# The Mixer's last projection as seven block products, with weight sums made by adding transfers and row loads issued by SyncE

## The chip, the cores and the metric

The kernel runs on one core of one Trainium2 chip. The metric is the device time of one execution in microseconds, as the median of several runs. Engines are named as in the profile: PE is the matrix engine, DVE the vector engine, ACT the scalar engine, POOL GpSimd, SP SyncE, which here issues transfers only.

## The reference, cut to what matters

A trunk layer over 1024 tokens of 1024 channels, in fp32: a mixing sub-layer with two convolution branches, then a gated FFN, each behind a norm and inside a residual. The part around the change:

```python
y_a = jnp.einsum('bsc,cd->bsd', y_a, w_short_out[l])
...
y_b = jnp.einsum('bsc,cd->bsd', u, w_conf_out[l])
g_a, g_b = jnp.split(jax.nn.sigmoid(gate_br), 2, axis=-1)
mix = jnp.einsum('bsd,de->bse', g_a * y_a + g_b * y_b, w_o[l])
x = x + g1 * mix
h2 = rms_norm(x, norm_ffn_g[l]) * (1.0 + sc2) + sh2
a, bgate = jnp.split(jnp.einsum('bsd,df->bsf', h2, w_ffn_in[l]), 2, axis=-1)
x = x + g2 * jnp.einsum('bsf,fd->bsd', jax.nn.silu(a) * bgate, w_ffn_out[l])
```

The vectors `g1`, `sc2`, `sh2` and so on come from `silu(c) @ w_ada + b_ada`, the modulation.

## The kernel before, in words

Activations lie in SBUF with channels on the 128 partitions and tokens along them: 8 rows of channels (`j`) by two halves of 512 tokens (`h`). A matmul multiplies a 128x128 weight block with a 128x512 operand into one PSUM bank.

**fp32 out of three passes.** Each operand is split in a high part and a rest (`split`, L543; `t_split`, L552: a cast on ACT and a subtraction on DVE). So is each weight tile of 128x1024, 512 KB (`split_w`, L234: `wh` by ACT at L244, `wl` by DVE or POOL at L245). `mm3` (L495) then makes three matmuls: wh with xh, wh with xl, wl with xh.

**Seven block products.** Nearly all projections take their matrix in duals: a dual is four weight blocks 11, 12, 21, 22, and its four result blocks are made by seven products instead of eight, the Strassen-Winograd scheme (`PRODUCTS`, the names "1", "2", "6", "5", "7", "3", "4"; `product`, L512). Products 6, 5, 7 and 3 take sums of weight blocks, and 6, 5, 7, 3 and 4 take sums or differences of operand blocks. A product is 24 matmuls. Weights are planned in the list `plan`, and `next_w` (L466) keeps three units begun: the one that is handed out and `AHEAD` = 2 more (`fetch`). In the duals of the second output product (`conf_units`) and of the first, a sum of two weight blocks is a load by SP and an adding transfer onto it, issued by POOL. In the first duals of the FFN (`dual_units`, L251, `begin` at L272 for the second) the sums are made by DVE.

**The stages around the change**, each bound to its order on PE:
- ya, `w_short_out`: two duals, then the gated result stands in the tiles `ma[j, h]`. In it also runs the layer norm of the other branch, on DVE and ACT.
- yb, `w_conf_out`: two duals in `CONF_ORDER`. `yb_evac` (L1391) multiplies the result with the gate rows `gb` (loaded by POOL, `gates_b`) and adds it onto `ma`: by DVE for row 1, half 0 of each block (L1402), by an adding transfer `ma<-gb` of POOL for the others (L1403), twelve in all.
- mix, `w_o`: the one projection that is done directly. `mix(i, h)` (L1463) runs over two halves and eight column blocks: one weight tile and 24 matmuls (`col_block`) each, 384 in all. In the first half the last three weight tiles are kept (`KEPT`) for the second, so that there are 13 loads. Each block loads its rows of x by POOL (`xr`, L1466), evacuates with `x1 = gate*out + xr` on DVE (L1471), stores x1 to DRAM by POOL (L1474), squares it on ACT (L1475) and adds the square to the half's sum on DVE (L1481). Also here run ten of the modulation's blocks, each a load by SP and a multiply with accumulation on DVE (`load_b`, L486).
- The norm before the FFN: `norm_2_first` (L1499) for half 0 after the first block of half 1. Its sum over channels (`parts_sum`) is two matmuls, `ss` at L689, between a split of the sum (`sumh`, `suml`, L682 and L683) and the inverse root on DVE. `norm_2_half` and `norm_2_sums` do half 1 and the operand sums of the FFN's first two duals, on DVE.
- the FFN's first projection, `w_ffn_in`, in eleven duals in `in_order`; its head is the time of the first two.

The order of each engine's instructions is the order of the program, with some moved behind a named instruction (`tc.issue_after`).

Of the kernel before, what the change touches and what calls it, by code (L numbers as in the profile page):

```python
# [40 lines left out]
P = 128  # L41
# [50 lines left out]
S2_AT = (2, 3, 4)  # L92
# [28 lines left out]
CONF_ORDER = [(d, m) for m in "1256" for d in range(2)] + [(0, "3")] + [(d, m) for m in "74" for d in range(2)] + [(1, "3")]  # L121


MOD_FROM = 16

# [14 lines left out]
def block_kernel(ctx: ExitStack, tc: tile.TileContext, x0, xT, c, vecs, ada, w_first, w_plain, w_duals,  # L140
# [110 lines left out]
    def dual_units(mats, n, early=0, eng=nc.vector):  # L251
# [20 lines left out]
        def begin():  # L272

            with tc.issue_after(load.ins):
                get("21", "22")
            yield
            with tc.issue_after(parts.lo):
                eng.tensor_tensor(a["22"], a["21"], a["22"], ALU.add)
            with tc.issue_after(load.ins):
                get("11")  # L280
            yield
            a["s2"] = s2p.tile([P, T], F32, tag="x1", name="s2")[:, :n]
            with tc.issue_after(mix.half_0):
                eng.tensor_tensor(a["s2"], a["11"], a["22"], ALU.add)
            yield
# [70 lines left out]
    def added_units(mats):  # L356


        a = {}
        mat = dict(zip(("11", "12", "21", "22"), mats))  # L360

        def add(raw, b):
            nc.gpsimd.dma_start(raw, mat[b], accum_op=ALU.add)
            return raw

        def unit(m):
            if m == "6":
# [11 lines left out]
            return split_w(raw, 1024)  # L379

        return {m: (lambda m=m: unit(m)) for m in PRODUCTS}
# [3 lines left out]
    def conf_units(mats, d):  # L385
# [15 lines left out]
        def unit(m):  # L401
            if m == "5":
                raw = a["s1"] = add(get("22"), "21")
            elif m == "6":
                lo = split_w.lo
                raw = a["s2"] = get("11", (rawp, rawbp)[d])
                with tc.issue_after(lo):
                    nc.vector.tensor_tensor(raw, raw, a["s1"], ALU.add)
            elif m == "7":
                raw = add(get("21"), "11")  # L410
            elif m == "3":
                raw = add(a["s2"], "12")
            else:
                raw = get({"1": "11", "2": "12", "4": "22"}[m])
            return split_w(raw, 1024, () if m in "12" else (split.act, split.ins))

# [46 lines left out]
    plan += [(w_o[k], 1024) for ks in (range(KC), SECOND[KEPT:]) for k in ks]  # L463
    ready = []

    def next_w(ahead=AHEAD):  # L466

        fetch(ahead + 1)
        return ready.pop(0)
# [73 lines left out]
    def split(src, tile_of, name):  # L543
        hi, lo = tile_of(name + "h", dt=F32R), tile_of(name + "l", dt=F32R)
        split.act = nc.scalar.copy(hi, src).ins
        split.ins = nc.vector.tensor_tensor(lo, src, f32(hi), ALU.subtract).ins
# [5 lines left out]
    def t_split(src, hi, lo):  # L552
# [3 lines left out]
    def minus(out, a, b):  # L556

        nc.vector.scalar_tensor_tensor(out=out, in0=a, scalar=-1.0, in1=b, op0=ALU.mult, op1=ALU.subtract)
# [54 lines left out]

    kept = []

    def first_w(k):

        w = next_w(min(AHEAD, KC - 1 - k))
        if k >= KC - KEPT:
            kept.append(w)  # L620
        return w

    def second_w(i):

        if i < KEPT:
            fetch(i)
            return kept.pop(0)
        return next_w()
# [615 lines left out]
    n_mod = 0  # L1244
    for d, m in win_order:
# [22 lines left out]
        for n in range('55'.count(m) * (BEGUN < d < GATED)):  # L1268
            with tc.issue_after(short_conv.ins):
                modulation_of(MOD_FROM + n_mod, load(ada[MOD_FROM + n_mod], home=(dual_units.home,dual_units.home)[n_mod % 2]))  # L1270
            n_mod += 1
    while late:
        late.pop(0)()

# [11 lines left out]
    def z_split(m, k, src):  # L1286
        tz[m][k] = split(src, hl_tile, "z" + m)
# [24 lines left out]
    def load_b(i):  # L1312

        loaded.append((i, load(ada[i])))
        if len(loaded) > 1:
            with tc.issue_after(split.ins):
                modulation_of(*loaded.pop(0))


# [4 lines left out]
    loaded = []  # L1324
# [45 lines left out]
    for i, (d, m) in enumerate(ya_order):  # L1370
        gates_a(d, m)
        product(ya_banks[d], m, tq[m], ya_evacs[d], onto="2")
        if q_steps:
            q_steps.pop(0)()
        if i == 0:
# [10 lines left out]
    mg = [[None, None] for _ in range(KC)]  # L1386

    def mg_split(o, h):
        mg[o][h] = split(ma[o, h], hl_tile, f"mg{o}{h}")

    def yb_evac(d, banks):  # L1391
# [3 lines left out]
        def out(i, row, h, op, src):  # L1395
            j = 4 * d + 2 * i + row
            g = gbs.pop((j, h))
            op(g, src, g)
            if (row, h) == (1, 0):
                nc.vector.tensor_tensor(ma[j, h], ma[j, h], g, ALU.add)  # L1400
                mg_split(j, h)
            else:  # L1402
# [39 lines left out]
    def z_3(k):  # L1442
# [6 lines left out]
        (0, "4"): lambda: [mg_split(j, 0) for j in range(0, KC, 2)],  # L1449
# [9 lines left out]

# [3 lines left out]
    def mix(i, h):  # L1463
        j = SECOND[i] if h else i
        xr = g_tile("xr")
        nc.gpsimd.dma_start(xr, xT[j, :, halves[h]])  # L1466
        (o,) = col_block((second_w if h else first_w)(i), mg, (h,), "mix", SECOND if h else [*range(0, KC, 2), *range(1, KC, 2)])
        if h == 0:
            x1[j] = ucp.tile([P, T + CK - 1], F32, tag="uc", name=f"x1{j}")[:, :T]
        dst = x1[j][:, halves[h]]  # L1470
        evac = nc.vector.scalar_tensor_tensor(out=dst, in0=o, scalar=modc(16 + j), in1=xr, op0=ALU.mult, op1=ALU.add)  # L1471
        if (i, h) == (KC - 1, 0):
            mix.half_0 = evac.ins
        nc.gpsimd.dma_start(x1_dram[j][:, halves[h]], dst)  # L1474
        sq = nc.scalar.activation(xr, dst, AF.Square, scale=1.0 / 32.0)  # L1475
        if (i, h) == (KC - 1, 1):
            load_rsqrt(sq.ins)
        if i == 0:
            sums[h] = xr
        else:  # L1480
            mix.add = nc.vector.tensor_tensor(sums[h], sums[h], xr, ALU.add).ins  # L1481

    def h2_of(k, h, r2, hi_lo=None):

        t = x1[k][:, halves[h]]
        nc.vector.scalar_tensor_tensor(out=t, in0=t, scalar=aff2[:, k : k + 1], in1=r2, op0=ALU.mult, op1=ALU.mult)
        if hi_lo:
            hi, lo = hi_lo
            nc.scalar.activation(hi, t, AF.Identity, bias=modc(24 + k))
            nc.vector.scalar_tensor_tensor(  # L1490
                out=lo, in0=t, scalar=modc(24 + k), in1=f32(hi), op0=ALU.add, op1=ALU.subtract
            )
# [5 lines left out]
    def norm_2_first():  # L1498

        ss, hl = ps_tile("ss"), parts(sums[0])  # L1500
# [3 lines left out]
        r2 = rstd_end(*rstd_start(ss, eps1, "r2"))  # L1504
        for k in range(KC):
            ts["12"[k // KH]][k % KH] = hl = t_pair(f"h2{k}")
            h2_of(k, 0, r2, hl)
# [3 lines left out]
    def norm_2_half(k, r2):  # L1511
# [8 lines left out]
        t_split(t2[k], *ts["6"][k])  # L1520

    def norm_2_sums(m):

        b12, b22 = ([x1[k + i][:, halves[1]] for k in range(KH)] for i in (0, KH))
        b21 = [x1[k + KH][:, halves[0]] for k in range(KH)]
        with tc.issue_after(t_split.ins), tc.issue_after(t_split.act):
            if m == "7":
                for k in range(KH):
                    nc.vector.tensor_tensor(b12[k], b22[k], b12[k], ALU.subtract)
            los = []  # L1530
            for k in range(KH):
                if m == "4":
                    with tc.issue_after(los[k - 2]) if k > 1 else ExitStack():
                        minus(b21[k], t2[k], b21[k])
                ts[m][k] = t_pair("t" + m)
                t_split({"5": x1[k][:, halves[0]], "7": b12[k], "3": b22[k], "4": b21[k]}[m], *ts[m][k])
                los.append(t_split.ins)
# [7 lines left out]
    sums = {}  # L1545
    for h in range(2):
        for i in range(KC):
            mix(i, h)
            if h == 0:
                mg_split(i, 1)  # L1550
                for b in [32 + i] + [MOD_FROM + n_mod + i] * (MOD_FROM + n_mod + i < 32):
                    load_b(b)
            if (h, i) == (0, KC - 1):
                modulation_of(*loaded.pop())
            if h == 1 and i == 0:
                for k in range(KC):
                    affine(aff2, k, 32, vec, V_GFFN)
                norm_2_first()
            if h == 1 and i in S2_AT:
                next(in_units[1]["begin"])  # L1560


    in_order = [(0, "1"), (0, "2"), (1, "1"), (1, "2"), (2, "1")] + [(d, m) for d in range(2) for m in PRODUCTS[2:]]
    in_order += [(d, m) for d in range(2, N_IN) for m in PRODUCTS if (d, m) != (2, "1")]

    def in_unit(d, m):
# [9 lines left out]
        if (d, m) == (0, "6"):  # L1576
            with tc.issue_after(mix.add):
                return in_units[d][m](rstd_end.ins)
        return in_units[d][m]()

    plan += [lambda d=d, m=m: in_unit(d, m) for d, m in in_order]
    ha = {}
# [19 lines left out]
    def in_evac(d):  # L1602
        def evac(p, m, ps):
# [4 lines left out]
            elif m == "2":  # L1608
                nc.vector.tensor_tensor(ha[f, "1"], ps, ha[f, "1"], ALU.add)
# [83 lines left out]
    in_product(0, "1", norm_2_start)  # L1693
    r2 = rstd_end(*r2)
    for i, (d, m) in enumerate(in_order[1:5]):
        norm_2_half(i, r2)
# [309 lines left out]
```

## Time and profile before

| | |
|---|---|
| median of 3 runs | 1443.17 us (1442.23 to 1444.0) |
| profiled execution, its own time | 1443.7 us |
| its span | 1441.9 us |
| mean granted TensorE clock | 0.998 |
| chain that ended last, share of PE | 97% |
| DVE, ACT, POOL busy | 83%, 45%, 36% |
| the 16 DMA engines: queue of SP, queue of POOL | 30.6%, 25.6% |

The span goes from the first to the last recorded instruction; 1.8 us of the execution's own time lie around it. A row of a group has the code line, the engine, the operation, out<-in by the program's names, the tile, the count, busy us and the mean ns of one, then the idle time before it and what ended that. A row of waits has the instruction, what it waited for, the us in total, how often, and the longest. A row of a timeline has start and length in us. PEld is PE's loading of weights, which runs beside its matmuls. Where instructions follow each other without a gap their ends overlap, so the spacing of the starts is shorter than the duration.

### The profile page before, as it was taken

The numbers are of one execution on the slowest core, as the hardware profiler recorded it, in microseconds if no ns is written. First come the engines' busy times: TensorE is split into PE (matmuls) and PEld (weight loads), VectorE is DVE, ScalarE is ACT, GpSimd is POOL, SyncE is SP. The second block draws the span as 40 slices with busy tenths as digits, with TensorE's granted clock in tenths as the row PEclk, the third lists the DMA queues.
The fourth block names the chain that finished last, engine by engine and source line by source line (L and its number), as shares of the span: only waits on it lengthen the run. The fifth ranks groups of instructions, "written<-read, shape, count | busy, mean of one in ns | idle before, by whom it ended". The sixth has DMA issues, their size and how long they took to land.

```text
span 1441.9 us, 17770 instructions
## 1 busy us (share of the span) xinstructions
PE 1428.6 (99%) x6322; PEld 1173.5 (81%) x6322; DVE 1198.8 (83%) x1665; ACT 655.2 (45%) x963; POOL 522.0 (36%) x512
## 2 busy tenths in 40 slices
PE   8999999999999999999999999999999999999997
PEld 4888888888888888888888888888888888888887
DVE  7996999999899999989988898877777665866676
ACT  4873333333343457567426474533444443321235
POOL 0017777777677562013311001110111015563405
PEclk9999999999999999999999999999999999999999
DMA  9743233333335578768886248645555449996903
GB/s 349 282 162 90 72 117 117 103 117 103 132 124 183 161 244 296 219 193 203 223 317 228 79 141 267 205 149 186 185 175 161 138 143 358 389 372 191 340 0 117
DMA packets 95946, 275.04 MB, mean 191 GB/s; under 512 B 10945, under 2 KB 12993, under 8 KB 95858
## 3 DMA queue, kind: packets, MB, share of 16 engines
q1 hardware_dynamic: 46672, 148.92, 30.6%
q0 software_dynamic: 44000, 111.36, 25.6%
q10 hardware_dynamic: 5186, 13.64, 2.5%
q8 instruction: 49, 0.80, 0.2%
q14 instruction: 39, 0.32, 0.1%
HBM read 203.09 MB, written 67.63 MB: 188 GB/s over the span
## 4 chain that ended last, share of the span: by engine, by line
PE 97%; POOL 1%; DVE 0%; issue 0%; POOLq 0%
PE bank L506 14%; PE bank L505 14%; PE bank L508 14%; PE x L508 8%; PE x L506 8%; PE x L505 8%; PE z L506 4%; PE z L508 4%; PE z L505 4%; PE y L508 3%; PE y L506 3%; PE y L505 3%; PE mix L506 2%; PE mix L508 2%; PE mix L505 2%; PE lead L501 1%
## 5 line engine op out<-in xcount | busy, mean ns | idle before, releaser
L244 ACT CAST wh<-raw 128x1024 fp32r<-128x1024 f32 (+2 forms) x254 | 263.0, 1037 | 394.7 <-PE bank L506 138.1
L245 DVE TENSOR_TENSOR wl<-raw,wh 128x1024 fp32r<-128x1024 f32 (+2 forms) x176 | 212.4, 1208 | 38.1 <-ACT wh L244 35.5
L245 POOL TENSOR_TENSOR wl<-raw,wh 128x1024 fp32r<-128x1024 f32 x78 | 194.4, 2500 | 91.1 <-ACT wh L244 90.1
L1168 DVE SCALAR_TENSOR_TENSOR c<-diff,vec,c 128x512 f32<-128x512 f32 x232 | 163.4, 749 | 1.5
L1644 POOL DMA_DIRECT2D hid<-stage x70 | 37.4, 535 | 343.3 <-DVE stage L554 326.8
L505 PE MATMUL bank<-th,wh 128*128 128x512 f32 x336 | 130.7, 389 | 0.0
L506 PE MATMUL bank<-tl,wh 128*128 128x512 f32 x336 | 130.7, 389 | 0.0
L508 PE MATMUL bank<-th,wl 128*128 128x512 f32 x336 | 130.7, 389 | 0.0
L505 PEld LDWEIGHTS bank<-th,wh 128*128 128x128 f32 x336 | 63.1, 188 | 13.2
L508 PEld LDWEIGHTS bank<-th,wl 128*128 128x128 f32 x336 | 63.1, 188 | 13.1
L506 PEld LDWEIGHTS bank<-tl,wh 128*128 128x128 f32 x336 | 63.1, 188 | 13.0
L553 ACT CAST stage<-g 128x512 fp32r<-128x512 f32 x60 | 37.3, 622 | 74.7 <-DMA hid<-stage 41.0
L506 PE MATMUL x<-tl,wh 128*128 128x512 f32 x176 | 68.5, 389 | 0.0
L505 PE MATMUL x<-th,wh 128*128 128x512 f32 x176 | 68.5, 389 | 0.0
L508 PE MATMUL x<-th,wl 128*128 128x512 f32 x176 | 68.4, 390 | 0.0
L1168 DVE SCALAR_TENSOR_TENSOR c<-u,wsum,c 128x512 f32<-128x512 f32 x96 | 66.8, 750 | 0.8
L554 DVE TENSOR_TENSOR stage<-g,stage 128x512 fp32r<-128x512 f32 x60 | 41.2, 688 | 27.9 <-ACT stage L553 27.7
L1668 POOL DMA_DIRECT2D th<-hid x77 | 41.1, 534 | 52.2 <-PE x L508 26.4
L1668 POOL DMA_DIRECT2D tl<-hid x77 | 41.2, 535 | 19.6 <-DMA tl<-hid 5.6
L265 DVE TENSOR_TENSOR raw<-raw 128x1024 f32<-128x1024 f32 (+1 forms) x15 | 17.8, 1188 | 36.4 <-DMA raw<-in_w_fi 24.1
L486 DVE CUSTOM_DVE_ANT_0 raw<-raw,cs,vec 128x1024 f32<-128x1024 f32 x24 | 39.1, 1639 | 9.5 <-DMA raw<-in_ada 5.4
L505 PE MATMUL bank<-t2h,wh 128*128 128x512 f32 x112 | 43.6, 389 | 0.0
(833 smaller groups left out, 4143.1 us busy)
## 6 DMA issues: line engine op xcount, KB each, us to landing
hid<-stage POOLq DMA_DIRECT2D x70, 512.0 KB, 4.8
raw<-in_w_duals SPq DMA_DIRECT2D x65, 512.0 KB, 3.6
raw<-in_w_fi SPq DMA_DIRECT2D x54, 512.0 KB, 4.3
th<-hid POOLq DMA_DIRECT2D x77, 256.0 KB, 6.0
tl<-hid POOLq DMA_DIRECT2D x77, 256.0 KB, 6.0
ada<-in_ada SPq DMA_DIRECT2D x24, 512.0 KB, 5.9
raw<-in_ada SPq DMA_DIRECT2D x24, 512.0 KB, 4.7
raw<-in_w_fo SPq DMA_DIRECT2D x16, 512.0 KB, 6.1
```

The lines of the kernel that those rows point to most:

```text
L244: hi = nc.scalar.copy(wh, raw)
L245: lo = lo_engine.tensor_tensor(wl, raw, f32(wh), ALU.subtract)
L265: eng.tensor_tensor(a["s1"], a["21"], a["22"], ALU.add)
L486: nc.vector.tensor_tensor_reduce(out=raw, in0=raw, in1=cs, scale=1.0, scalar=col(V_ADA, b), op0=ALU.mult, op1=ALU.add, accum_out=modc(b),)
L505: nc.tensor.matmul(ps, wh, xh, start=first, stop=False, skip_group_check=again)
L506: nc.tensor.matmul(ps, wh, xl, start=False, stop=False, skip_group_check=again)
L508: mm3.ins = nc.tensor.matmul(ps, wl, xh, start=False, stop=last, skip_group_check=again).ins
L553: t_split.act = nc.scalar.copy(hi, src).ins
L554: t_split.ins = nc.vector.tensor_tensor(lo, src, f32(hi), ALU.subtract).ins
L1168: tap.ins = nc.vector.scalar_tensor_tensor(out=out, in0=src[:, s : s + H], scalar=wt, in1=acc, op0=ALU.mult, op1=ALU.add).ins
L1644: nc.gpsimd.dma_start(hid_dram[key], s)
L1668: nc.gpsimd.dma_start(t, hid_dram[key][:, s])
```

## The change

- `w_o` is laid out in duals. `mix` becomes two duals of seven products, 336 matmuls, in `MIX_ORDER` (products 1, 2, 6, 7, 4, 5, 3, each for both duals). It has 24 evacuations instead of 16: the products that close a part of a block add onto x1 (`mix_evac`, with `ngm`, the negative gate, for row 1).
- `mix_units` makes all its weight sums by adding transfers: product 6 loads block 11 and adds 21 and 22, product 3 adds 12 onto the same tile, 7 is 21 and 11, 5 is 22 and 21. The FFN's first two duals use the same units, so DVE's weight sums there go.
- The operand differences of product 6 are made by DVE (`m_6`), and added onto the blocks for products 7 and 4 by adding transfers (`onto`: `ma<-t2m`, `x<-t2`). Three of the sums of squares are `onto` too.
- In yb ten of the sixteen adds onto `ma` are DVE's now (four before); six adding transfers remain.
- `xr` is loaded by SP, one product ahead of its use. Five of mix's ten modulation blocks move into ya.
- The first norm's sum stands on PE ahead of product (1,"5"), behind (0,"5"); its rows are scaled after (1,"5"), (0,"3") and (1,"3"). `norm_2_start` of the second half moves from product (0,"1") of the FFN to (1,"1"), which now comes second in `in_order`.

POOL's order from the end of yb into mix, before (`gb` is a gate row, `ma` the merged operand, `x_dram` the store of x1):

```order
L1403 DMA ma_5145<-gb 128x512
L1403 DMA ma_5161<-gb 128x512
L1431 DMA gb<-gate_b_122 128x512
L1431 DMA gb<-gate_b_124 128x512
L1466 DMA xr<-in_xT 128x512 x4
L1403 DMA ma_5192<-gb 128x512
L1403 DMA ma_5207<-gb 128x512
L1466 DMA xr<-in_xT 128x512
L1474 DMA x_dram_5949<-x_5994 128x512
```

And now (`raw<-in_w_o` at L436 adds a weight block, `ma<-t2m` at L604 adds the difference of product 6):

```order
L1472 DMA gb<-gate_b_122 128x512
L1472 DMA gb<-gate_b_124 128x512
L436 DMA raw<-in_w_o 128x1024 x5
L604 DMA ma_4695<-t2m 128x512
L604 DMA ma_4758<-t2m 128x512
L436 DMA raw<-in_w_o 128x1024
L604 DMA ma_5006<-t2m 128x512
L604 DMA ma_5252<-t2m 128x512
L604 DMA ma_4709<-t2m 128x512
L1515 DMA x_dram_5964<-x_6072 128x512
```

The row loads are gone from POOL; six adds of weight blocks and eight of operands stand in their place, the weights' ahead of the operands'.

DVE's order at the first norm sum, before (`suml` is the rest of the split sum, `r2t` and `r2r` the inverse root):

```order
L1471 SCALAR_TENSOR_TENSOR x_6301<-mix_6276,mod,xr 128x512
L1481 TENSOR_TENSOR xr<-xr 128x512
L683 TENSOR_TENSOR suml<-xr,sumh 128x512
L278 TENSOR_TENSOR raw<-raw 128x1024
L1471 SCALAR_TENSOR_TENSOR x_6223<-mix_6316,mod,xr 128x512
L245 TENSOR_TENSOR wl<-raw,wh 128x1024
L569 SCALAR_TENSOR_TENSOR r2t<-r2r 128x512
```

And now (the first two rows evacuate product (1,"4"), the rows with `x_6311` and `x_6325` product (0,"5")):

```order
L1540 SCALAR_TENSOR_TENSOR x_6368<-bank,ngm,xr 128x512
L1540 SCALAR_TENSOR_TENSOR x_6382<-bank,ngm,xr 128x512
L1525 TENSOR_TENSOR xr<-xr 128x512
L251 TENSOR_TENSOR wl<-raw,wh 128x1024
L1525 TENSOR_TENSOR xr<-xr 128x512
L1540 SCALAR_TENSOR_TENSOR x_6311<-y,ngm,x_6311 128x512
L713 TENSOR_TENSOR suml<-xr,sumh 128x512
L1540 SCALAR_TENSOR_TENSOR x_6325<-y,ngm,x_6325 128x512
L251 TENSOR_TENSOR wl<-raw,wh 128x1024
L615 SCALAR_TENSOR_TENSOR r2t<-r2r 128x512
```

Between the last evacuation that feeds the sum and `suml` there are now a second add, a weight split and an evacuation of the next product.

The diff, cut to its core:

```diff
-S2_AT = (2, 3, 4)
+NORM_2_AT = (1, "5")
+NORM_2_ROWS = {(1, "5"): (0, 1, 2, 3), (0, "3"): (4, 5), (1, "3"): (6, 7)}
...
+MIX_ORDER = [(d, m) for m in "1267453" for d in range(2)]
+MOD_LATE, MOD_YA, MOD_MIX = (30, 40), range(1, 11), range(4, 10)
...
+    def mix_units(mats, d):
...
+        def get(*blocks, home=None):
...
+            raw = load(mat[blocks[0]], home=home)
+            for b in blocks[1:]:
+                add(raw, b)
+            return raw
+        def add(raw, b):
+            conf_adds.append(nc.gpsimd.dma_start(raw, mat[b], accum_op=ALU.add).ins)
+        def unit(m):
+            if m == "6":
+                raw = a["s2"] = get("11", "21", "22", home=(rawp, rawbp)[d])
+            elif m == "3":
+                raw = a["s2"]
+                add(raw, "12")
+            else:
+                raw = get(*{"1": ("11",), "2": ("12",), "7": ("21", "11"), "4": ("22",), "5": ("22", "21")}[m])
+            return split_w(raw, 1024, (split.act, split.ins))
...
-    plan += [(w_o[k], 1024) for ks in (range(KC), SECOND[KEPT:]) for k in ks]
+    mix_w = [mix_units([w_o[d, m] for m in range(4)], d) for d in range(2)]
+    plan += [mix_w[d][m] for d, m in MIX_ORDER]
...
-            if (row, h) == (1, 0):
+            if d or (row, h) == (1, 0):
                 nc.vector.tensor_tensor(ma[j, h], ma[j, h], g, ALU.add)
...
-            else:
+            elif d == 0:
                 nc.gpsimd.dma_start(ma[j, h], g, accum_op=ALU.add)
...
-        nc.gpsimd.dma_start(xr, xT[j, :, halves[h]])
+            nc.sync.dma_start(xrs[j, h], xT[j, :, halves[h]])
...
+        elif h and j % 2:
+            mix.add = onto(sums[h], sq)
...
+        def m_6(k):
+            nc.vector.tensor_tensor(b[0, 1][k], b[0, 0][k], b[0, 1][k], ALU.subtract)
+            t2m[k] = hl_tile("t2m", F32)
+            minus(t2m[k], b[0, 1][k], b[1, 1][k])
+            for r in range(2):
+                onto(b[r, 0][k], t2m[k])
+            tm_split("6", k, t2m[k])
...
+            if (d, m) == NORM_2_AT:
+                norm_2_first()
+            product(banks[d], m, tm[m], evacs[d], onto="2")
+            if (d, m) in NORM_2_ROWS:
+                norm_2_rows(NORM_2_ROWS[d, m])
...
-        nc.vector.tensor_tensor(b11, b11, b12, ALU.subtract)
+        nc.vector.tensor_tensor(b12, b11, b12, ALU.subtract)
         t2.append(hl_tile("t2", dt=F32))
-        minus(t2[k], b11, b22)
+        minus(t2[k], b12, b22)
+        for i in (k, k + KH):
+            onto(x1[i][:, halves[0]], t2[k])
...
-    in_units = [dual_units([w_fi[d, m] for m in range(4)], 1024, EARLY[d]) for d in range(N_IN)]
+    in_units = [mix_units([w_fi[d, m] for m in range(4)], d) if d < 2 else dual_units([w_fi[d, m] for m in range(4)], 1024, EARLY[d]) for d in range(N_IN)]
...
-    in_order = [(0, "1"), (0, "2"), (1, "1"), (1, "2"), (2, "1")] + [(d, m) for d in range(2) for m in PRODUCTS[2:]]
+    in_order = [(0, "1"), (1, "1"), (0, "2"), (2, "1"), (1, "2")] + [(d, m) for d in range(2) for m in PRODUCTS[2:]]
...
-    in_product(0, "1", norm_2_start)
+    in_product(0, "1")
+    in_product(1, "1", norm_2_start)
```

More of the change, by code (lines that the diff above doesn't have):

```diff
@@ L272, in begin @@
         def begin():
+            a["s2"] = s2p.tile([P, T], F32, tag="x1", name="s2")[:, :n]
             with tc.issue_after(load.ins):
-                get("21", "22")
+                nc.sync.dma_start(a["s2"], mats[0])
             yield
[L277 to L284, printed above, removed]
+            for b in (2, 3):
+                nc.gpsimd.dma_start(a["s2"], mats[b], accum_op=ALU.add)
             yield
@@ L1267, in block_kernel, with late_modulation @@
             q_steps.pop(0)()
[L1268 to L1271, printed above, removed]
+        if m == "5":
+            for n in range(2 * (BEGUN < d < GATED)):
+                with tc.issue_after(short_conv.ins):
+                    modulation_of(MOD_FROM + n_mod, load(ada[MOD_FROM + n_mod], home=dual_units.home))
+                n_mod += 1
     while late:
         late.pop(0)()
+    later, whole = list(range(*MOD_LATE)), []
+    def late_modulation(behind, more, tile_of):
+        if whole:
+            with tc.issue_after(behind):
+                modulation_of(*whole.pop())
+        if more and later:
+            whole.append((later.pop(0), tile_of()))
+            with tc.issue_after(load.ins):
+                nc.sync.dma_start(whole[0][1], ada[whole[0][0]])
     tz = {m: [None] * KH for m in PRODUCTS}
@@ L1461, in block_kernel, with xr_loads @@
     x1_dram = [dram.tile([P, T], F32, name=f"x1_dram{j}") for j in range(KC)]
-    def mix(i, h):
-        j = SECOND[i] if h else i
-        xr = g_tile("xr")
-        nc.gpsimd.dma_start(xr, xT[j, :, halves[h]])
-        (o,) = col_block((second_w if h else first_w)(i), mg, (h,), "mix", SECOND if h else [*range(0, KC, 2), *range(1, KC, 2)])
-        if h == 0:
-            x1[j] = ucp.tile([P, T + CK - 1], F32, tag="uc", name=f"x1{j}")[:, :T]
+    sums, xrs = {}, {}
+    def xr_loads(d, m):
+        row, h = {"2": (0, 0), "6": (0, 1), "7": (1, 1), "4": (1, 0)}.get(m, (0, None))
+        for i in range(2 * (h is not None)):
+            j = 4 * d + 2 * i + row
+            xrs[j, h] = g_tile("xr")
+            nc.sync.dma_start(xrs[j, h], xT[j, :, halves[h]])
@@ L1577, in in_unit @@
             with tc.issue_after(mix.add):
-                return in_units[d][m](rstd_end.ins)
+                return in_units[d][m]()
         return in_units[d][m]()
     plan += [lambda d=d, m=m: in_unit(d, m) for d, m in in_order]
+    h2_of.lo = None
+    ngm = cp.tile([P, KC], F32, name="ngm")
+    nc.vector.tensor_scalar(ngm, mod[:, 16:24], -1.0, None, ALU.mult)
+    mix()
+    assert not later and not whole
+    raws[:] = [rawp] * 3 + [rawbp] * 2
     ha = {}
@@ L1608, in evac @@
             elif m == "2":
[L1609 removed]
+                with behind(d, norm_2_half.scaled[p]):
+                    nc.vector.tensor_tensor(ha[f, "1"], ps, ha[f, "1"], ALU.add)
             elif m == "7":
```

203 lines of the change are left out of this document (122 added, 81 removed).

## The prediction

> **What bounds the kernel now.** I read the page's busy times first, then TensorE's waits, then the stages around the change as windows, then VectorE (DVE) and the transfers in those stages. The page's head:
>
> ```profile
> span 1441.9 us, 17770 instructions
> PE 1428.6 (99%) x6322; PEld 1173.5 (81%) x6322; DVE 1198.8 (83%) x1665; ACT 655.2 (45%) x963; POOL 522.0 (36%) x512
> ```
>
> The view of TensorE's (PE's) waits has three rows in all, each of something that happens once:
>
> ```profile
> PE clock L721 <- ACT sq L668: 1.9, 1, 1.9
> PE clock L721 <- DVE ones_r L739: 1.6, 1, 1.6
> PE clock L721 <- DVE newton L780: 0.7, 1, 0.7
> ```
>
> So PE is the bound, nearly without a gap, and matmuls taken out of its stream count in full unless another engine is then late. Whether one is, the four stages tell: first output product (ya), second (yb), the last projection (mix), and the head of the FFN. The columns are the window, its length, busy us of PE, PE's weight loads, DVE, ACT and POOL with their counts, the granted clock, the share of the 16 DMA engines, GB/s:
>
> ```profile
> 555.00:633.00 78.00, 78.00 (x340) 63.45 (x339) 69.89 (x102) 48.33 (x74) 5.23 (x6) 1.00 0.79 237
> 633.00:711.00 78.00, 78.00 (x343) 63.84 (x342) 74.51 (x109) 48.91 (x74) 21.65 (x30) 1.00 0.81 203
> 711.00:798.20 87.20, 87.20 (x386) 72.16 (x385) 70.04 (x105) 39.16 (x56) 19.12 (x34) 1.00 0.76 264
> 798.20:876.00 77.80, 77.80 (x343) 63.86 (x342) 70.41 (x94) 47.35 (x71) 4.32 (x8) 1.00 0.44 137
> ```
>
> DVE has 8 us left in ya, 3.5 in yb, 17 in mix. ACT, at most 63% busy, is far from any bound.
>
> **PE: what is removed.** The first row is the tile view of mix's first matmul, the others are PE's timeline: the norm's only matmuls inside the stage, and the FFN's first matmul:
>
> ```profile
> L505 PE MATMUL mix<-mg00h,wh x8: 389/389/389, 711.3 to 749.3; 128*128 128x512 f32 x8
> 760.21 0.40 PE L689 MATMUL ss<-sumh,ones_c 128*128 128x512 f32 x1
> 760.45 0.39 PE L689 MATMUL ss<-suml,ones_c 128*128 128x512 f32 x1
> 798.79 0.39 PE L505 MATMUL x<-h20h,wh 128*128 128x512 f32 x1
> ```
>
> From 711.3 to 798.79 are 87.5 us. Less 0.5 for the two ss matmuls (0.24 between their starts), 384 matmuls take 87.0, 0.2266 us each. Fourteen products of 24 are 336: 48 fewer, **-10.9 us**. One product is then 5.44 us, the stage 76.3. That the change might not do this is excluded by PE's order, which has 48 rows fewer. Nothing else on PE changes in number.
>
> **DVE: what is added.** The groups of the mix stage (count | busy, mean ns | idle before, released by), then spacing from DVE's timeline (a row with x2 or x3 is a run):
>
> ```profile
> L245 DVE TENSOR_TENSOR wl<-raw,wh 128x1024 fp32r<-128x1024 f32 x13 | 15.9, 1221 | 0.4 <-ACT wh L244 0.2
> L486 DVE CUSTOM_DVE_ANT_0 raw<-raw,cs,vec 128x1024 f32<-128x1024 f32 x10 | 12.7, 1281 | 0.0
> L1471 DVE SCALAR_TENSOR_TENSOR x<-mix,mod,xr 128x512 f32<-128x512 f32 x15 | 11.2, 750 | 9.6 <-PE mix L508 9.6
> 654.42 1.89 DVE L1295 TENSOR_TENSOR cv<-cv 128x512 f32<-128x512 f32 x3
> 612.57 2.35 DVE L245 TENSOR_TENSOR wl<-raw,wh 128x1024 fp32r<-128x1024 f32 x2
> 741.23 0.75 DVE L1471 SCALAR_TENSOR_TENSOR x<-mix,mod,xr 128x512 f32<-128x512 f32 x1
> 741.89 1.22 DVE L245 TENSOR_TENSOR wl<-raw,wh 128x1024 fp32r<-128x1024 f32 x1
> ```
>
> Instructions overlap at their ends, so one in a row costs its spacing: 0.60 us for 128x512 (from 1.89 for three), 1.13 for 128x1024 (from 2.35 for two), 0.66 for a PSUM evacuation (741.23 to 741.89), 1.28 for a modulation. By counts from the diff and DVE's order:
> - ya gets five modulations: 69.9 + 6.4 = 76.3 of 78.0.
> - yb gets six adds of ma that were transfers: 74.5 + 3.6 = 78.1 of 78.0.
> - mix loses five modulations (6.4), three weight sums for the FFN (3.4), three sums of squares (1.8, now transfers) and one wl (1.1), and gets eight evacuations (24 for 16: 5.3), twelve operand splits (7.2) and eight differences for product 6 (4.8): 70.0 - 12.7 + 17.3 = 74.6 of 76.3.
> - The FFN head loses seven weight sums and eight operand sums: 70.4 - 7.9 - 4.8 = 57.7 of 77.8. No gain on PE, which does not wait there.
>
> Over ya, yb and mix DVE has 229.0 us of work in 232.3; it had 214.4 in 243.2. The 3.3 us left are the narrowest thing in this change. A little lateness is hidden: a weight tile is asked for two products ahead, so wl has some us of lead. Where PE asks directly, it is not.
>
> That place is the first norm sum. Before, its DVE chain was:
>
> ```profile
> 754.97 0.75 DVE L1471 SCALAR_TENSOR_TENSOR x<-mix,mod,xr 128x512 f32<-128x512 f32 x1 [3.25 <-PE mix L508]
> 756.47 0.69 DVE L1481 TENSOR_TENSOR xr<-xr 128x512 f32<-128x512 f32 x1 [0.75 <-ACT xr L1475]
> 757.85 0.69 DVE L683 TENSOR_TENSOR suml<-xr,sumh 128x512 fp32r<-128x512 f32 x1 [0.69 <-ACT sumh L682]
> ```
>
> From the evacuation to suml 3.6 us, with PE asking at 760.21, 1.7 us after suml's end. In the new order PE asks after product (0,5), one product (5.44 us) behind the tile (1,4) that closes the sum; between that evacuation and suml DVE has a wl and an evacuation of (0,5) as well: 3.6 + 1.1 + 0.7 = 5.4. Nothing is left to hide lateness that DVE brings along. ss is in PE's own queue, so all matmuls behind it wait. Bounds: nothing, if DVE is on time; 5.4, one product, if it comes with the lag that the full yb stage can leave. I take the middle, **2.7 us**.
>
> The five modulations of ya fit into its 8 us; should they not, yb inherits up to 6.4 us of lag, which is rival B.
>
> **Transfers.** Issue rows (count, KB, median us from issue to landing) and the queues:
>
> ```profile
> q1 hardware_dynamic: 46672, 148.92, 30.6%
> q0 software_dynamic: 44000, 111.36, 25.6%
> raw<-in_w_conf SPq DMA_DIRECT2D x12, 512.0 KB, 4.3
> raw<-in_w_conf POOLq DMA_DIRECT2D x6, 512.0 KB, 6.7
> raw<-in_w_short POOLq DMA_DIRECT2D x6, 512.0 KB, 6.4
> raw<-in_w_duals POOLq DMA_DIRECT2D x4, 512.0 KB, 5.8
> ma<-gb POOLq DMA_DIRECT2D x12, 256.0 KB, 6.1
> xr<-in_xT POOLq DMA_DIRECT2D x16, 256.0 KB, 5.3
> ```
>
> The POOL weight rows and ma<-gb are adding transfers. Product 6 now needs a load and two adds, one after the other: 4.3 + 6.7 + 6.7 = 17.7 us, and 2.3 for its split (ACT cast and DVE rest): 20.0. The look-ahead is three products, 16.3 us. If the first load started only then, PE would wait 3.7 us, once in mix and once in the FFN head (the second dual follows in the same pipeline). But SyncE issues as soon as the buffer is free, and POOL's order has five of the six adds for the mix's products 6 and 7 in a row ahead of the operand adds: I take 0 and keep 3.7 + 3.7 for the range. [...] POOL is then held for these adds, with the operand adds ma<-t2m behind them: those land by the 6.1 us row, and product 7 wants them two products after they are made, 10.9 us: hidden unless a wait of over 4.8 us stands ahead of them.
>
> The rows of x (xr) go to SyncE, one product ahead. A wait there for a free tile would hold the w_o and modulation loads behind it by up to one product, 5.4 us; with 4.3 for landing and 2.3 for splitting that is 12 of 16.3 us: hidden. POOL saves their issue; it is 36% busy, so nothing for the sum.
>
> How full are the 16 engines? Plain: 30.6% of 1441.9 us over 148.92 MB is 2.96 us a MB, so 1.55 for 512 KB and 0.78 for 256 KB. q0 takes 369.1 us; at the plain price its 99.8 MB of plain bytes take 295.5, and the other 73.6 us are its 11.53 adding MB (sixteen 512 KB, twelve 256 KB): 6.4 a MB, estimates of 3.35 and 1.67. Mix after: 12 w_o and 5 modulation loads 26.4, 16 xr and 16 stores 25.0, ten adds of weights 33.5, eleven of 256 KB 18.4: 103 us, in a stage of 76.3. Before, the same working gives 61 against 66 measured (0.76 x 87.2). yb has 14.8 us free and loses six ma<-gb, 10.0, so 25 us of w_o can go there; the stores and the last sums may trail into the FFN head, which goes from 34 (0.44 x 77.8) to 34 + 33.5 + 13.4 - 7.8 = 73 of 77.8. Together about as much as there is. I take no wait for it; its price is rival C.
>
> **Sum.** Profiled execution 1443.7 (span 1441.9 and 1.8 around it) - 10.9 + 2.7 = 1435.5. The median of the runs, 1443.17, is 0.5 below the profiled one: **1435.0**.
>
> **The rivals.** A change of under 0.2% (2.9 us) is what a measurement of this kernel cannot tell from none: faster means below 1440.3, slower above 1446.1.
>
> A, forecast: 1433 to 1438, one short stall at the norm sum. 0.58.
>
> D: no stall, 1432.3. For it: DVE waited for PE here, so it has slack at the right moments:
>
> ```profile
> DVE x L1471 <- PE mix L508: 9.6, 5, 3.2
> DVE wl L245 <- ACT wh L244: 4.4, 3, 3.2
> DVE xr L1481 <- ACT xr L1475: 3.0, 4, 0.8
> DVE ma L870 <- DMA ga<-gate_a: 1.9, 1, 1.9
> ...
> DVE vz L867 <- PE bank L508: 0.2, 1, 0.2
> ```
>
> Against: that slack is spent on 17.3 us of new work. 0.17.
>
> B: DVE becomes the bound of ya to mix. Beside its 229.0 us of work it has waits of its own on ACT and transfers (4.2 in the rows on ACT above, without the 3.2 that PE's buffers caused there, and 1.9 and less in nine smaller rows, 8 more: 12 at most, of which I take 9 to 12, since some fell where DVE had nothing else). 238 to 241 in 232.3 makes 5.7 to 8.7: 1438 to 1441. 0.13.
>
> C, slower: the 16 DMA engines become the bound of mix. With the 5 us of prefetch that the stage held, 108 us of transfers stand in 76.3. If all 25 us of yb's room are used, PE is 7 us late (1439); if half, 20 (1452); if none, 32. It decides above 10.9 us that find no room outside. For it: adds can't start before their first load has landed, and the second of a tile not before the first add. [...] Against it: such fullness has stood here without any wait of PE:
>
> ```profile
> 738.00:750.00 12.00, 12.00 (x54) 9.95 (x53) 10.50 (x24) 2.67 (x4) 1.65 (x4) 1.00 0.99 364
> ```
>
> 0.12, of which 0.09 above 1446.
>
> **How the numbers follow.** The range goes from D less the scatter of the median (1431.6) to A with both 3.7 us terms of the adds, 1442.4, and a little of C: 1443. It leaves out most of C. Faster: A, D, most of B, 0.82; same 0.09; slower 0.09.
>
> **What would show it.** PE's waits: a row at ss (the first norm sum) of 0 to 5 us is A; rows at "wh" or "wl" behind raw<-in_w_o or raw<-in_w_fi by DMA are the adding chain or C, with a DMA share near 1.0 in mix; many small waits on DVE's wl in yb and mix are B, with DVE over 97% there. The mix stage should last 76.3 us plus its stalls. I am wrong if PE waits over 10.9 us in all, or if the FFN head, where I cost nothing, holds the larger wait.

## The result, and the profile after

The changed kernel is slower: 1466.18 us median of 4 runs (1460.71 to 1469.92) against 1443.23 (1442.23 to 1444.0), ratio 1.0157 with a 95% interval of 1.014 to 1.0175. Its profiled execution took 1463.86, the span is 1462.1.

The head of its page, and PE's share of the chain that ended last (97% before):

```profile
span 1462.1 us, 17798 instructions
...
PE 1428.6 (98%) x6274; PEld 1167.8 (80%) x6274; DVE 1203.9 (82%) x1681; ACT 666.3 (46%) x980; POOL 541.7 (37%) x529
...
PE 76%; DVE 8%; DMA 7%; issue 4%; POOL 2%; ACT 2%; POOLq 0%; SPq 0%; DVEq 0%; ACTq 0%
```

PE has 48 matmuls fewer and the same 1428.6 us of busy time: those left were slower somewhere. Its waits sum to 24.5 us, the five largest rows below; before there were only the three rows that the prediction shows, 4.2 us:

```profile
PE bank L539 <- ACT wh L250: 5.8, 2, 5.6
PE bank L719 <- ACT sumh L712: 5.2, 1, 5.2
PE bank L539 <- DVE x L1540: 2.4, 1, 2.4
PE x L542 <- DVE wl L251: 2.2, 2, 1.3
PE ss L725 <- DVE sq L1523: 1.9, 1, 1.9
```

The windows are ya with yb, mix from its first matmul to the FFN's first, and the FFN's head (columns as in the prediction, the last three being clock, DMA share, GB/s):

```profile
555.00:715.20 160.20, 158.27 (x683) 127.18 (x683) 152.94 (x228) 96.90 (x148) 24.78 (x34) 1.00 0.80 225
715.20:811.60 96.40, 83.19 (x339) 67.08 (x338) 70.67 (x104) 42.22 (x63) 26.26 (x35) 0.93 0.96 259
811.60:890.00 78.40, 72.86 (x313) 57.81 (x312) 63.31 (x88) 51.61 (x82) 19.82 (x26) 1.00 0.89 223
```

Mix lasted 96.4 us instead of the 76.3 that its matmuls need. By the first matmul of mix the kernel was 4 us behind before's (715.4 against 711.3), by the FFN's first matmul 13 (811.9 against 798.79), at the end 20. In mix the share of the 16 DMA engines rose from 0.77 to 0.96, in the FFN head from 0.44 to 0.89. The first half of mix, in steps of 15 us:

```profile
725.00:740.00 15.00, 15.00 (x68) 12.43 (x67) 9.53 (x14) 5.95 (x10) 8.51 (x10) 1.00 1.04 235
740.00:755.00 15.00, 9.39 (x40) 7.48 (x39) 7.21 (x10) 6.84 (x12) 5.15 (x7) 0.95 1.09 229
755.00:770.00 15.00, 12.59 (x46) 9.88 (x45) 11.38 (x20) 5.98 (x10) 0.86 (x1) 0.84 0.93 301
```

The share adds up the times of all packets; in the first two windows it is 1.04 and 1.09, so times of packets overlap there. By it the engines are full, and they move little (235 and 229 GB/s; the full window of before, at 0.99, moved 364): in these windows POOL's adding transfers are under way. What that did to landing times, from the issue rows (median us from issue to landing):

```profile
raw<-in_w_o SPq DMA_DIRECT2D x12, 512.0 KB, 7.3
raw<-in_w_o POOLq DMA_DIRECT2D x10, 512.0 KB, 9.3
xr<-in_xT SPq DMA_DIRECT2D x16, 256.0 KB, 7.7
ma<-t2m POOLq DMA_DIRECT2D x8, 256.0 KB, 11.1
```

Against 5.1 for the loads of `w_o`, 6.7 for adding weights, 5.3 for the rows of x and 6.1 for adding operands before. POOL's timeline shows how they follow each other (start, length, in brackets the wait before):

```profile
706.69 1.63 POOL L1472 DMA_DIRECT2D gb<-gate_b  x3 [5.05 <-DMA ma<-gb]
708.29 0.95 POOL L436 DMA_DIRECT2D raw<-in_w_o  x1
718.05 1.76 POOL L436 DMA_DIRECT2D raw<-in_w_o  x2 [8.80 <-DMA raw<-in_w_o]
728.95 1.74 POOL L436 DMA_DIRECT2D raw<-in_w_o  x2 [9.14 <-DMA raw<-in_w_o]
730.03 2.44 POOL L604 DMA_DIRECT2D ma<-t2m  x2
...
744.52 0.85 POOL L604 DMA_DIRECT2D ma<-t2m  x1 [2.49 <-DMA raw<-in_w_o]
```

No `w_o` add was issued before 708 us, so the free room of yb, on which the prediction had counted, went unused (share 0.77 from 633 to 711). Two orders kept them out. POOL has them behind the gate rows and sums of yb. And the load that the first add goes onto was itself issued late:

```profile
699.14 0.33 SPq L234 DMA_DIRECT2D raw<-in_w_o  x1
```

SyncE had waited for a weight split on DVE to free the tile, and the load landed 5.4 us later, at 704.6. So POOL's own order held the first add for under 4 us. From there on POOL twice waited some 9 us for the landing of an add, with the operand adds behind. The last operand that product (0,"7") needs was split on ACT at 751.2, with a square, another split and a weight cast behind it in order, and PE stood 5.6 us.

### The profile page after: what moved, and what is told of

Same layout as the page of the kernel before. It is cut to its first block, busy times and chain, and to the rows that moved or that the text cites. A ratio compares the mean times of both kernels' runs of the same rounds, so it can differ in the third digit from the quotient of the medians.

```text
span 1462.1 us, 17798 instructions
## 1 busy us (share of the span) xinstructions
PE 1428.6 (98%) x6274; PEld 1167.8 (80%) x6274; DVE 1203.9 (82%) x1681; ACT 666.3 (46%) x980; POOL 541.7 (37%) x529
## 4 chain that ended last, share of the span: by engine, by line
PE 76%; DVE 8%; DMA 7%; issue 4%; POOL 2%; ACT 2%; POOLq 0%; SPq 0%; DVEq 0%; ACTq 0%
PE bank L540 11%; PE bank L539 11%; PE bank L542 11%; PE x L540 8%; PE x L542 8%; PE x L539 8%; PE z L542 4%; PE z L539 4%; PE z L540 4%; PE y L540 2%; PE y L542 2%; PE y L539 2%; DMA ma<-t2m 1%; DVE wl L251 1%; DMA raw<-in_w_o 1%
## 5 line engine op out<-in xcount | busy, mean ns | idle before, releaser
L520 DVE CUSTOM_DVE_ANT_0 ada<-ada,cs,vec 128x1024 f32<-128x1024 f32 x34 | 42.7, 1280 | 6.9 <-DMA ada<-in_ada 6.7
L540 PE MATMUL bank<-t2l,wh 128*128 128x512 f32 x112 | 43.6, 389 | 0.0
```

Of the source, the lines that this page charges most:

```text
L520: nc.vector.tensor_tensor_reduce(out=raw, in0=raw, in1=cs, scale=1.0, scalar=col(V_ADA, b), op0=ALU.mult, op1=ALU.add, accum_out=modc(b),)
L540: nc.tensor.matmul(ps, wh, xl, start=False, stop=False, skip_group_check=again)
```

## The experiments

Theory **T**: the 16 engines are full of adding transfers, so that everything in flight lands late. Rivals: **O**, the order (POOL issues after landings, ACT and DVE stand in order behind), **Q**, SyncE's queue held by row loads, **V**, DVE has too much work, **L**, only the landing of the operand adds matters. Each time stands against runs of the kernel before on the same chip.

### Weight blocks overwritten instead of added

```diff
         def add(raw, b):
-            conf_adds.append(nc.gpsimd.dma_start(raw, mat[b], accum_op=ALU.add).ins)
+            conf_adds.append(nc.gpsimd.dma_start(raw, mat[b]).ins)
```

> Leaves out the sums of weight blocks in the last projection and in the FFN's first two duals: the twenty transfers that add a block onto a tile overwrite it instead, so the products use single blocks; all transfers, waits and their order stay. Theory T, the 16 DMA engines are the bound (share 0.96 from the first matmul of mix to its end): an adding transfer of 512 KB costs the engines about 1.8 us more than a plain one (3.35 against 1.55), twenty of them 36 us, so most of the 20 us over before goes; 1440 to 1450, adds landing in 5 us instead of 9. Rival O, the order: what costs is that POOL issues one after another's landing and ACT and DVE stand in order behind; the waits stay, 1458 to 1466. Rival V, DVE has too much work: no change, 1460 to 1470.

1449.48 us (ratio 1.0039, 1.0029 to 1.005): 17 of the 23 us are gone though the transfers, their order and what waits for what are the same. POOL's queue took 28.6% of 16 engines' span instead of 30.0%:

```profile
span 1443.5 us, 17798 instructions
...
q0 software_dynamic: 47472, 121.06, 28.6%
```

That is 412.8 us of engine time against 438.6, so adding costs 1.3 us more than overwriting for each of the twenty 512 KB. The time is in T's range, at its upper end, and not in O's. But the overwriting transfers of `w_o` also landed sooner (7.2 us against 9.3, where 5 had been expected), and with that POOL's waits for landings shrank too. So this run shows that the adding costs the time; it does not part full engines from POOL's order. In PE's waits the first norm sum stayed:

```profile
PE bank L719 <- ACT sumh L712: 5.4, 1, 5.4
```

### Rows of x by POOL again

```diff
-            nc.sync.dma_start(xrs[j, h], xT[j, :, halves[h]])
+            nc.gpsimd.dma_start(xrs[j, h], xT[j, :, halves[h]])
```

> The rows of x are loaded by POOL again, everything else as changed. In the changed kernel SyncE stood up to 13.3 us at a row load that waited for a free tile, with weight and modulation loads behind it. Rival Q, SyncE's queue is the cause: without these waits weight loads land earlier, 1450 or below. Theory T: the same bytes at the same time, within 4 us of the changed kernel (1460 to 1470). POOL's own queue then holds the row loads behind adds that wait for landings, so slower than 1470 is possible for rival O.

1465.59 us, as changed, so SyncE's long waits at row loads are not what costs the 23 us, and Q is out as the main cause. That they cost nothing at all is not shown: mix took 100.5 us here instead of 96.4, with 9.4 us of wait ahead of (0,"7") instead of 5.6, and a gain on SyncE can be hidden in that.

### Operand adds of mix by DVE

```diff
             for r in range(2):
-                onto(b[r, 0][k], t2m[k])
+                nc.vector.tensor_tensor(b[r, 0][k], b[r, 0][k], t2m[k], ALU.add)
```

> The eight operand adds of product 6 in mix (ma<-t2m, 256 KB each, landing after 9.6 to 11.0 us) are made by DVE instead of by adding transfers. Theory T: takes 8 x 1.67 = 13 us off the 16 engines in mix and the 5.6 us stall at product (0,7) goes with the slow clock behind it (1.6 us); about 7 to 10 us faster, 1453 to 1459. Rival V: adds 4.8 us to DVE, slower or the same, 1463 to 1475. Rival O: the stall at (0,7) goes, but no other; 1456 to 1460.

1451.0 us (1.005, 1.003 to 1.007), 15 better, more than T and O had expected. Its mix stage:

```profile
713.40:798.80 85.40, 79.52 (x340) 64.24 (x339) 74.89 (x112) 42.82 (x64) 19.25 (x27) 0.98 0.93 271
```

DVE does 4.2 us more than in the changed kernel, in a stage 11 us shorter: against V.

### The same bytes, with nobody waiting for them

The kernel above, and on POOL in the same places two plain transfers for each add, to scratch:

```diff
+                for n in range(2):
+                    nc.gpsimd.dma_start(dram.tile([P, H], F32, name=f"spare{k}{r}{n}"), t2m[k])
```

> As the kernel with the operand adds on DVE (1451 us), but POOL issues sixteen plain transfers of the same tiles (256 KB each, to scratch in DRAM that nothing reads) in the places where the adding ones stood: about the same time on the 16 engines (16 x 0.78 = 12.5 us against 13.4), on the same queue, but nobody waits for their landing. Theory T, the full engines delay whatever is in flight: the adds of weight blocks and the loads get late again, 1457 to 1466. Rival L, what costs is that ACT and DVE wait in order for the landing of the operand adds: the time stays at 1449 to 1453.

1460.78 us (1.0123, 1.0106 to 1.014): 10 of the 15 us come back. Mix as a window is full again (0.96):

```profile
713.50:807.90 94.40, 84.07 (x340) 67.24 (x339) 75.01 (x112) 42.39 (x64) 27.70 (x43) 0.91 0.96 289
```

PE's longest wait is now one for weights, and DVE made that split late, behind a modulation block whose load took 12.6 us to land (3.9 at most at this place in the run above):

```profile
PE bank L542 <- DVE wl L251: 5.5, 2, 3.7
763.55 1.28 DVE L520 CUSTOM_DVE_ANT_0 ada<-ada,cs,vec 128x1024 f32<-128x1024 f32 x1 [3.91 <-DMA ada<-in_ada]
```

L is out as the whole cause: two thirds come back though nobody waits for these landings, and at this wait by a load that lands late. But the sixteen issues also hold POOL (27.7 us busy against 19.2), and `w_o` adds stand behind them in its order. In the run above POOL issued four in a row (first line below); here, with the transfers to scratch (`spare<-t2m`) between them, the third of the four came 14.6 us later:

```profile
727.30 3.53 POOL L436 DMA_DIRECT2D raw<-in_w_o  x4 [9.24 <-DMA raw<-in_w_o]
...
727.83 1.75 POOL L436 DMA_DIRECT2D raw<-in_w_o  x2 [9.43 <-DMA raw<-in_w_o]
728.91 3.91 POOL L1565 DMA_DIRECT2D spare<-t2m  x6
...
743.02 0.89 POOL L436 DMA_DIRECT2D raw<-in_w_o  x1 [0.73 <-ACT mg7h L580]
```

The adds themselves landed no later than in the run above (median 9.4 us against 9.5). So the run does not part the engines' share, T, from POOL's order, O; of the rivals O stays open as a part of the cause.

### Weight sums made early, in DRAM

All sums of weight blocks for mix and the FFN's first two duals are made in DRAM during the input projection, and later loaded plainly:

```diff
+            with tc.issue_after(load.ins):
+                nc.sync.dma_start(made_steps[0][1], made_steps[0][2])
...
+            with tc.issue_after(pool_los[-1][1]):
+                nc.gpsimd.dma_start(t, more, accum_op=ALU.add)
```

> All weight sums of mix and of the FFN's first two duals are made by adding transfers in DRAM during the input projection, where the DMA engines were busy 0.2 to 0.4; later each product needs one plain load. Theory T: mix loses 10 adding transfers (33.5 us) and gets back 6 plain ones (9.3): its transfers fall from 103 us to 79, and with a buffer no longer held from product 6 to product 3 the loads come earlier. The stalls at (0,7) and of the last two thirds of mix and in the FFN head shrink: 1438 to 1450. Rival O: the same, since the chain of issue after landing goes too (this run does not part T from O). Rival V: 1458 or more, since DVE's work is unchanged. If the early transfers disturb the input projection, PE's waits appear before 555 us.

1449.3 us (1.0042, 1.0026 to 1.0058), as T and O had both expected. Mix and FFN head are nearly free of waits but for the two norm sums (3.9 and 1.1 us), though mix still took 84 us. In the profiled run, the slowest of the five at 1457.45, mix begins at 727.0, 12 us later than in the changed kernel: most of that is lost in the input projection, where the early sums are made.

### Both, with the early sums sooner

One add at every second product, from the first one on, and the operand adds on DVE.

> The operand adds of mix on DVE and the weight sums of mix and FFN head made early in DRAM, these now from the start of the input projection at every second product, where POOL and the engines had more room, and ended before 350 us. Theory T: mix has 103 - 33.5 + 9.3 - 13.4 = 66 us of transfers in 76, so its stalls go but for the first norm sum; the input projection is undisturbed: 1434 to 1442, faster than before. Rival V: DVE with 4.8 us more in mix keeps some stalls, 1440 to 1448. Rival: the early sums disturb the input projection wherever they stand, 1445 to 1452.

1442.78 us (0.9993, 0.998 to 1.0005): no difference from before. Mix took 77.2 us, with DVE busy for 75.2 and hardly a wait of PE, so V is out there:

```profile
718.60:795.80 77.20, 77.07 (x340) 63.40 (x340) 75.23 (x113) 43.55 (x66) 10.28 (x17) 1.00 0.71 233
```

What is left is lost ahead of mix, which begins at 718.6, 7 us later than before. This trace is 1.3 us ahead at 230 us, then loses 4.6 in the input projection, where PE waits for POOL's weight splits (1.5 us in all) and for ACT (1.4), and 4.1 in ya and yb.

### The first norm's sum one product later

On the kernel with operand adds on DVE.

```diff
-NORM_2_AT = (1, "5")
+NORM_2_AT = (0, "3")
```

> As the kernel with the operand adds on DVE (1451 us), and the first norm's sum one product later on PE, ahead of (0,"3") instead of (1,"5"), its rows scaled after (0,"3") and (1,"3"). Theory N, DVE is late at that sum: the stall there (2.7 us, and 1 us of slow clock behind it) goes: 1446 to 1448. Rival: the rows are scaled one product later too and are late for the FFN's first product, so that the stall moves behind the last product of mix: 1450 to 1455.

1459.8 us (1.0113, 1.0091 to 1.0136), 9 slower: PE still waited 1.9 us at the sum, and 5.6 in the FFN's first product for a scaled row. The rival's mechanism, at twice its highest price; some of that is chance, since in the profiled runs mix began 3.7 us later here (717.2 against 713.4), though the two kernels are the same up to there.

### Operand adds of the FFN head by DVE

> As the kernel with the operand adds of mix on DVE (1451 us), and the eight operand adds in the FFN head (x<-t2) on DVE as well. The engines' share in that head was 0.90. Theory T: 13 us of transfers less, the small waits there (about 2 us in all for t2 and wl) fall by 1 to 2: 1448 to 1451. Rival V: DVE is asked for 4.8 us more in the head, where it had 65 of 80, no change or up to 2 us slower.

1454.67 us (1.0085, 1.0068 to 1.0102), 3.7 slower than without; PE waits up to 1.8 us for operand splits there (0.8 without). That speaks for V in this place. It is not shown: in the profiled runs the head and what follows took 2.8 us longer, and another 2.8 were lost ahead of mix, which the edit does not touch.

### Early sums where POOL stands idle, and the squares on DVE

First the early sums only at products 3 and 4 of each dual, then also the sums of squares on DVE:

```diff
-        if n_win >= 0 and n_win % 2 == 0 and pool_los:
+        if m in "34" and pool_los:
             made_step()
...
-        elif h and j % 2:
-            mix.add = onto(sums[h], sq)
```

> As the kernel with the operand adds on DVE and all weight sums made early (1442.8 us; its mix stage took 77.2 us, but up to the first matmul of mix it was some 5 us behind), with the early sums issued only at products 3 and 4 of each dual of the input projection, where POOL stood idle for some 3 us between its weight splits. If the rest was POOL held by them: 1436 to 1440, faster than before. If it is the transfers' share of the engines there, wherever they stand: 1441 to 1445.

> As the kernel with the early sums at products 3 and 4, and the three sums of squares that were adding transfers (sq<-sq) on DVE again. PE waited 1.9 us at the second norm's ss for the last of these sums, and ran slowly for about 1 us after. If the landing of these transfers is that wait: 2 to 3 us faster than the kernel without this edit. If DVE is late there on its own: no difference, or up to 2 us slower, since DVE gets 1.8 us more.

1440.86 us (0.998, 0.9972 to 0.9989), between the two expectations; then 1439.27 us (0.9971, 0.996 to 0.9982), faster than both kernels. The gain of the second over the first, 1.6 us, is below the 2 to 3 expected and within their scatter, but the wait it was made for fell from 1.5 to 0.3 (1.9 in the run before these two). Mix and FFN head of the last one as windows:

```profile
716.30:793.70 77.40, 77.11 (x339) 63.22 (x339) 76.13 (x116) 42.74 (x64) 7.07 (x14) 1.00 0.65 222
793.70:873.70 80.00, 79.45 (x346) 64.52 (x346) 70.94 (x98) 55.45 (x87) 13.49 (x20) 1.00 0.65 191
```

Its PE waits at the places that had stalled, the FFN's operand splits, the second norm's sum and the first:

```profile
PE x L572 <- DVE t2l L628: 0.4, 1, 0.4
PE ss L757 <- DVE sq L734: 0.3, 1, 0.3
...
PE bank L751 <- ACT sumh L744: 0.3, 1, 0.3
```

Mix gives its whole 10 us. DVE is busy for 76.1 of 77.4, and PE hardly waits for it. Against that 5 us are lost ahead of mix (716.3 against 711.3): 1 in the input projection and 4 in ya and yb, as in the changed kernel.

Over the runs the length of mix goes with the time that its transfers took on the engines (share times window, worked out from the windows of each trace):

| kernel | engines' time in mix, us | length of mix, us |
|---|---|---|
| changed | 93 | 96.4 |
| bytes without wait | 91 | 94.4 |
| operand adds by DVE | 79 | 85.4 |
| blocks overwritten | 78 | 84.4 |
| sums made early | 69 | 84.1 |
| both, sums sooner | 55 | 77.2 |
| the last one | 50 | 77.4 |

In the run with 69 us the first norm sum was still 3.9 us late, with slow matmuls behind it. So taking the adding transfers out of mix gives the time back. How much of their cost is the full engines and how much the waits for landings in POOL's order, no run parts.

## Why the prediction was wrong

**PE, right.** 48 matmuls fewer are worth 10.9 us: with the adding transfers out of the way mix takes 77.4 us against the 76.3 of the working (76.6 if it is taken from first matmul to first matmul), and 87.5 before.

**Transfers, the step that failed.** The sum of the engines' work was near: some 103 us worked out for mix, 93 measured (0.96 of 96.4). The mistake is the sentence behind it, "I take no wait for it"; PE waited 24.5 us in all, where the prediction called itself wrong above 10.9. It moved 25 us of `w_o` transfers into yb, and none of the adds was issued before 708 us: the first load that they go onto came at 699.1, when a weight tile was free, and POOL's order, shown ahead of the prediction, has them behind yb's last gate rows. Rival C was this mechanism, at 0.12 and 1439 to 1464; its lower end rested on the same room in yb. Its chance was the larger error: 108 us of demand in 76 was the largest number of the whole working. That its price with no room in yb, 32 us, is close to the whole loss is in part luck: C puts all of it in mix, but 20 us were lost there, 7 in the FFN head and 4 ahead, and 6 of the 20 are the clock.

**Landing times.** The adding chain was costed at the medians of a stage whose share was 0.8 (6.7 and 6.1 us). At 0.96 on average they were 9.3 and 11.1. The nothing taken for product 6's chain of 20 us held all the same: PE began both its products in mix without a wait. But the operand adds, "hidden unless a wait of over 4.8 us stands ahead of them", were not hidden: the waits of 8.8 and 9.1 us did stand ahead of them. The share is not the whole of a landing time: with the operand adds on DVE it fell to 0.93, and the weight adds still took 9.5.

**The first norm sum.** 2.7 us were expected from DVE's own load, 5.2 came, and the reason is only partly that. With the sums made early and the squares on DVE it is 0.3, though DVE has more to do in mix (76.1 us against 70.7) in less time. In the overwriting run it was still 5.4 with the engines at 0.92. So what made DVE late there was mostly what it waited for, transfers among it (two modulation blocks came 3.6 and 2.6 us late); the parts of that were not measured apart. DVE's work in mix itself had been put too high, at 74.6 us.

**ya and yb.** Costed at nothing, they lost about 4 us in the profiled run, and 3 to 7 in every other trace of the changed kernel's kind, the last one's 4 among them. Most rows there are waits of 0.2 to 0.7 us for DVE's splits: rival B in small, seen but not tested. It is most of what still stands between the last kernel and the forecast.

**The FFN head** was costed at nothing with "73 of 77.8" on the engines; it lost 7. With the weight blocks overwritten it lost 2, with the sums made early and the squares on DVE 0.6, so most of that was the adding transfers too.

**The stalls' own sum.** In mix PE waited 5.6 + 2.4 + 5.2 = 13.2 us for some 20 us of loss. Most of the remainder is the clock, below: the slow matmuls behind these three waits add up to 6.0 us.

**The row loads.** Their wait on SyncE reached 13.3 us and not the 5.4 allowed. No run shows a cost of it: the time did not move when they left that queue.

## What to carry to other kernels

When a change turns engine work into transfers, add up the engine time of all transfers in the stage that has to hold them, and count room in an earlier stage only if the issuing queue's order and a free buffer let them be issued there. Sums of constant operands can be moved to where the DMA engines have room (a share of 0.28 to 0.36 in the changed kernel from 150 to 400 us, in the input projection); here that, with the sums of operands and squares back on DVE, turned a loss of 23 us into a gain of 4. A median landing time belongs to the stage in which it was measured: the adds of 512 KB landed in 6.7 us in yb before, and in 9.3 in mix.

## What the runs showed of the hardware

After its long waits PE ran slowly. Behind the 5.6 us stall, PE's timeline:

```profile
753.85 0.77 PE L539 MATMUL bank<-mg7h,wh 128*128 128x512 f32 x1 [5.61 <-ACT wh L250]
754.42 0.63 PE L540 MATMUL bank<-mg7l,wh 128*128 128x512 f32 x1
754.84 0.63 PE L542 MATMUL bank<-mg7h,wl 128*128 128x512 f32 x1
755.27 0.63 PE L539 MATMUL bank<-mg7h,wh 128*128 128x512 f32 x1
...
757.15 0.40 PE L542 MATMUL bank<-mg7h,wl 128*128 128x512 f32 x1
```

Starts are 0.43 us apart instead of 0.23 for the next seven matmuls, 1.5 us in all, and the granted clock was 0.84 in the window behind this stall (755 to 770 us, where the stall of 2.4 us lies too) and 0.77 in the one with the first norm sum's (785 to 800). In the traces of the changed kernel and of the runs, each of the eight waits of 3.7 us and more was followed by 7 to 14 such matmuls, 1.5 to 3.3 us. The six waits of 2.2 to 2.7 us were followed by 9 to 13. A single wait of 2.4 us was enough (the run with the sums made early, at 475.6). Most single waits of under 2 us cost 0.1 to 0.6, but short ones close behind another wait also slowed PE: in the run of the bytes without wait, one of 1.3 us, 2.5 us behind one of 1.5, was followed by seven slow matmuls. The prediction had left this out of the price of a stall: in mix it was 6.0 of some 20 us lost.

An adding transfer of 512 KB cost the 16 engines 1.3 us more than an overwriting one of the same bytes in the same place (438.6 against 412.8 us in POOL's queue, for twenty of them; what fuller engines add is in this figure).
